# The order of two heads in the products of probabilities by values, in a two-block transformer forward pass

## Chip, cores and metric

The kernel runs on one core of one Trainium2 chip. The metric is the device time of one execution in microseconds (us). The engines are TensorE (PE, with its weight loads shown apart as PEld), VectorE (DVE), ScalarE (ACT), GpSimd (POOL) and SyncE (SP), which issues most of the transfers.

## The reference, cut to what matters

The model is a chain of four layers over 512 tokens of width 1024, all in float32. A gated delta rule with a mixture of experts comes first, then a sparse attention (here called the first attention block) with a mixture of experts, then two equal layers that each hold a latent attention, a spatial gating unit and a banded attention. All three attentions end in the same product, probabilities by values, for each head:

```
s = jnp.einsum('bqhd,bkhd->bhqk', qi, k).astype(jnp.float32) * scale
s = jnp.where(mask[None, None], s, NEG_INF_2)
p = jax.nn.softmax(s, axis=-1).astype(v.dtype)
return jnp.einsum('bhqk,bkhd->bqhd', p, v)
```

A head is 64 wide in the value, so two heads fill 128 partitions of an output. There are 16 heads in the first attention block (in 4 groups of 4, each with two branches that need softmax over tokens, br = 0 and 1), and 8 in each latent and each banded attention.

## The kernel before

Tokens are cut into NT = 4 tiles of 128. Weights come in pieces of 512 KB and are split on chip into a high and a low part (L107 on ACT, L108 on DVE), and a projection is three matmuls for each block of weights (L112, L113, L114 in `mm3`). The tile that such a projection accumulates in carries the name mm or br, after its group of PSUM banks: four banks are called mm, two are called br, two are called tp.

`softmax_t` works on one head. For each of the four query tiles t it makes the scores (in the first attention block L1293 and L1294), takes the row's maximum on DVE (L1108), the exponential on ACT (L1110), scales on DVE (L1113 or L1115), transposes t + 1 blocks on PE (L187, tile tp) and copies them on ACT into PT (L1117). PT holds all probabilities of that head, transposed, and is three deep. Four mm banks serve the scores and the output of the product.

The product works on a pair of heads, u = 0 and u = 1, that share one PSUM bank `o`: head 0 writes its partitions 0 to 63 and head 1 partitions 64 to 127. For each key tile jt the rows of queries from jt on are taken, so the matmuls have 512, 384, 256 and 128 columns for jt = 0 to 3. Each such float32 matmul is two instructions in the trace, so a pair of heads has 16 instructions: 4 key tiles by 2 heads by 2. In the first attention block they are on L1299 (8 pairs by 2 branches, 16 groups, x256 instructions), in the other two attentions on L1578 (2 layers by 2 attentions by 4 pairs, 16 groups, x256). The first matmul of each head, at jt = 0, reads columns of PT that the last query tile writes, so it needs that head's whole softmax.

```
for jt in range(NT):
    for u_ in range(2):
        h = 2 * p + u_
        PE.matmul(o[u_ * 64:u_ * 64 + 64, jt * 128:], lhsT=vt[:, jt, h * 64:h * 64 + 64],
                  rhs=pt_rhs(PTs[u_], jt), start=jt == 0, stop=jt == NT - 1)
```

The program is written straight on, but a planner in the tile framework orders the instructions of each engine before the program runs. It goes by its own costs, takes what is ready, and among ready instructions the one that stands first in the program. In the trace the instructions on PE are mixed accordingly: between the scores and the transposes of a head there are pieces of projections that stand later in the program. In the latent attention `branch(0, p, ...)`, a gated projection, follows the product of pair p. In the banded attention the operands of the next pair, `banded(p + 1)`, stand between the softmax of a pair and its product for p < 3. In the first attention block only `queries(g + 1)`, for g < 3, is there to be mixed in, and a group of heads begins with the scores of compressed blocks (L1259, L1260, tile sc), a softmax over them (DVE L1269 to L1276, ACT L1271, tile pc), transposes, and the product that opens the output bank (L1284).

Of the kernel before, what the change touches and what calls it, by code (L numbers as in the profile page):

```python
# [19 lines left out]
T = 512  # L20
# [45 lines left out]
class Net:  # L66
# [24 lines left out]
    def chunk(self, src, n=RING, eng=None):  # L91
        """a piece of a weight, on chip as two float32r parts that sum to it"""
        nc = self.nc
        j, self.turn = self.turn, (self.turn + 1) % (RAW + len(self.more))
        raw = self.more[j - RAW] if j >= RAW else self.ring.tile([128, RING], F32, name="raw", tag="raw", bufs=RAW)
        nc.sync.dma_start(raw[:, :n], src)
        j, self.turn2 = self.turn2, (self.turn2 + 1) % (HL + len(self.pairs))
        if j >= HL:
            hi, lo = self.pairs[j - HL]
        else:  # L100
            hi = self.ring.tile([128, RING], F32R, name="hi", tag="hi", bufs=HL)
            lo = self.ring.tile([128, RING], F32R, name="lo", tag="lo", bufs=HL)
        self.split(hi[:, :n], lo[:, :n], raw[:, :n], eng)
        return hi, lo
# [11 lines left out]
    def phase(self, **banks):  # L116
        """PSUM banks by tag for the stretch of the program that follows"""
        if banks != self.banks:
            self.pool.close()
            self.banks = banks  # L120
            if banks:
                self.ps = self.pool.enter_context(self.tc.tile_pool(name="ps", bufs=1, space=bass.MemoryType.PSUM))
# [11 lines left out]
    def proj_t(self, chunks, xh, xl, evac, kt=8, tag="mm"):  # L134
        """y^T tiles of 128 columns by 512 tokens; chunks hold 4 k by 256 columns."""
        m = 0
        nk = kt // 4
        for p in range(len(chunks) // nk):
            pst = [self.psum(tag), self.psum(tag)]
            for kk in range(nk):  # L140
                hi, lo = self.chunk(chunks[p * nk + kk])
                for j in range(2):
                    for k in range(4):
                        s = slice(k * 256 + j * 128, k * 256 + j * 128 + 128)
                        kx = kk * 4 + k
                        self.mm3(pst[j], hi[:, s], lo[:, s], xh[:, kx], xl[:, kx], kx == 0, kx == kt - 1)
            for j in range(2):
                evac(m, pst[j])
                m += 1

    def proj_n(self, chunks, xh, xl, evac, kt=8, n=512, inner=None, early=False):
        """y tiles of 128 tokens by n columns; chunks hold 2 k by n columns. inner: the last block's token tiles
        end one after the other, and evac follows as many tiles behind; early: they start one after the other,
        as far as the weights' places go."""
        nk = kt // 2
        for b in range(len(chunks) // nk):
            pst = [self.psum() for _ in range(NT)]
            def part(t, kk, ch):
                hi, lo = ch
                for k in range(2):  # L160
                    kx = kk * 2 + k
                    ts = slice(t * 128, t * 128 + 128)
                    cs = slice(k * n, k * n + n)
                    self.mm3(pst[t][:, :n], xh[:, kx, ts], xl[:, kx, ts], hi[:, cs], lo[:, cs], kx == 0, kx == kt - 1)
            last = b == len(chunks) // nk - 1
            lag = NT
            m = HL if early and not b else 1
            if inner is not None and last:
                m, lag = nk, inner
            for k0 in range(0, nk, m):  # L170
                ks = range(k0, min(nk, k0 + m))
                ch = [self.chunk(chunks[b * nk + kk], 2 * n) for kk in ks]
                for t in range(NT):
                    for kk in ks:
                        part(t, kk, ch[kk - k0])
                    if t >= lag:
                        evac(b, t - lag, pst[t - lag][:, :n])
            for t in range(max(0, NT - lag), NT):
                evac(b, t, pst[t][:, :n])

    def transpose_tile(self, src, n, evac, tag="tp"):
        """n 128-wide blocks of src (128 rows) transposed, four to a bank; evac(first, count, psum)."""
# [7 lines left out]
    def to_xt(self, src, t, xh, xl, n=8, tag="tp"):  # L190
        """token tile t [128, n*128] -> columns t of xh/xl [128, n, 512]."""
# [11 lines left out]
    def deeper(self, pool, n):  # L203
        """n more places for split weights, in pool"""
# [6 lines left out]
    def longer(self, *tiles):  # L211
        """tiles as further places for weights in flight"""
# [4 lines left out]
    def rpow(self, out, in_):  # L217
        """out = in_ ** -0.5 (small tiles)."""
# [3 lines left out]
    def rows(self, src, n, tag, eng=None):  # L222
        """DRAM row [1, n] on every partition."""
# [4 lines left out]
    def rows_pe(self, src, tag):  # L228
        """rows, by the tensor engine"""
# [9 lines left out]
def gdn(net, xt, aside):  # L239
    """gated delta rule: returns (yh, yl), the operand of the output projection; aside(room) is work for its idle queues."""  # L240
# [4 lines left out]
    with ExitStack() as cx:  # L245
# [17 lines left out]
        def gate(p, tag="mm", more=lambda: None):  # L263
            """2 silu(z) of two heads, transposed"""
# [9 lines left out]
        with ExitStack() as c1:  # L274
# [13 lines left out]
            # decay and step of each token and head  # L288
# [31 lines left out]
            def conv_silu(c, ps, dst, eng):  # L320
                """dst = 2 silu(causal conv of 4 taps)"""
# [15 lines left out]
            def inv_norm(i, h, key, out):  # L337
                """out[:, h::8] = 1 / norm of head h's rows"""
# [7 lines left out]
            def k_head(h):  # L346
                """the strictly lower part of (beta k k^T) * decay of a head's chunks"""
# [28 lines left out]
            def later(f, lag):  # L376
                """f, once lag others have come after it"""
# [30 lines left out]
            # inverses of the unit lower triangular blocks of 32, then 64, then 128  # L408
# [96 lines left out]
        with ExitStack() as c2:  # L505
            p3 = c2.enter_context(tc.tile_pool(name="gdn3", bufs=1))
            def prep(t):
                """decays, and the operands that carry them"""
# [83 lines left out]
            def scaled(t, so, ops):  # L592
                """rows of the heads over their norms"""
# [14 lines left out]
            def output(t, y, yh, yl):  # L608
                """transposed, and gated by z"""
# [70 lines left out]
def mix_out(net, l, chunks, yh, yl, resid, rp, done):  # L680
    """LayerNorm(alpha * resid + y @ w); done(t, tile) gets each token tile"""
# [24 lines left out]
class Moe:  # L706
# [22 lines left out]
    def route(self, t, h):  # L729
        """h: token tile t after the LayerNorm; picks its experts and sends its rows to them"""  # L730
# [26 lines left out]
    def dispatch(self):  # L757
        """top-2 experts of the top group of each token; slots of the experts' first 128 tokens"""
# [15 lines left out]
        def first_max(src, n, oh):  # L774
            """src (n by 4) - max of four, the maximum negated; the one-hot of its first place into oh"""
# [9 lines left out]
        # the best two of every group, and the best group  # L785
# [18 lines left out]
        # columns: token and destination row of a slot, in parts that bfloat16 holds  # L804
# [31 lines left out]
    def overflow(self):  # L836
        """the experts of tokens beyond the first 128 of an expert, in tiles of 128"""
# [82 lines left out]
    def places(self):  # L920
        """room that is idle between the projection before and the end of the experts, for their weights"""
# [8 lines left out]
    def experts(self):  # L930
# [6 lines left out]
        def operand(e, n, tag, src):  # L937
            """n transposed blocks of an expert's rows as an operand, and the steps that make it, four blocks each"""
# [10 lines left out]
        def up(e, xh, xl, steps):  # L949
            """gated hidden rows; steps run between the pieces of the weights"""  # L950
# [46 lines left out]
    def combine(self, done):  # L997
        """LayerNorm(alpha * h + the experts' weighted rows) by token tiles, all over alpha"""
# [68 lines left out]
def bias_setup(net, room):  # L1067
    """the biases by distance, in DRAM: n_fwd from -527, s_fwd from -127 on. Made in room [16, 1712]"""
# [18 lines left out]
def toeplitz(net, pool, src, h, bufs=2):  # L1087
    """tiles[u][p, x] = src[h + u, p + x]: the bias of query p of a tile and the key x before the tile's end"""
# [6 lines left out]
def softmax_t(net, pool, score, tb, gate=None, scale=1.0):  # L1095
    """P^T of a head: P = softmax(scale * (scores + bias)) (* gate), causal by tiles of 128: block
    t + 3 j of the tile is key tile j by query tile t"""
# [28 lines left out]
def nsa(net, xt):  # L1126
# [4 lines left out]
    with ExitStack() as cx:  # L1131
# [88 lines left out]
        with ExitStack() as c2:  # L1220
# [3 lines left out]
            def queries(g):  # L1224
                """scaled queries of a group's heads, high parts on partitions 0-63, low on 64-127"""
# [12 lines left out]
            for g in range(4):  # L1238
# [11 lines left out]
                # compressed blocks: scores of four heads, transposed  # L1250
# [29 lines left out]
                for pr in range(2):  # L1280
# [5 lines left out]
                    for br in range(2):  # L1286
# [10 lines left out]
                        for jt in range(NT):  # L1297
                            for u in range(2):
# [56 lines left out]
class Second:  # L1355
# [8 lines left out]
    def pre(self, t, h, pool):  # L1364
        """rmsnorm of token tile t, transposed into the projections' operand"""
# [9 lines left out]
    def silu2(self, pool, dst, ps):  # L1375
        """dst = 2 silu(ps)"""
# [5 lines left out]
    def run(self, done):  # L1382
# [6 lines left out]
        with ExitStack() as cx:  # L1389
# [13 lines left out]
            def branch(n, p, y, emit, tag="br"):  # L1403
                """a quarter of branch n: its gated products' columns 256 p to 256 p + 255, transposed"""
# [15 lines left out]
            with ExitStack() as c0:  # L1420
                ap = c0.enter_context(tc.tile_pool(name="mla", bufs=1))
                # latent attention's operands
# [35 lines left out]
                def fetch(j):  # L1458
                    """a piece of the up projections; it stays while other weights pass"""
# [5 lines left out]
                def query(h):  # L1465
                    """operand of a head's queries, kept in DRAM"""
# [15 lines left out]
                def z_store(i, chunks, more):  # L1482
                    """2 silu of a gate's columns, kept in DRAM"""
# [7 lines left out]
                def keys(m):  # L1491
                    """keys of two heads, and a tile of all heads' values"""
# [27 lines left out]
            # spatial gating  # L1520
            ya = y_pair()
            with ExitStack() as c0:
# [28 lines left out]
                def mix(m, ps):  # L1551
                    """a quarter of the branch: its values mixed along the sequence, times u and the gate"""
# [17 lines left out]
            with ExitStack() as c2:  # L1570
                ap = c2.enter_context(tc.tile_pool(name="att", bufs=1))

                def pv_pair(PTs, vt, p, i, yf):
                    o = net.psum()
                    for jt in range(NT):
                        for u_ in range(2):
# [11 lines left out]
                def banded(p):  # L1588
                    """operands of two heads of the banded attention"""
# [179 lines left out]
```

## Time and profile before

| | |
|---|---|
| time, median of 3 runs | 2262.78 us (2261.91 to 2266.01) |
| span of the profiled execution, first to last instruction | 2254.8 us |
| between span and median | 8.0 us |
| PE busy | 2108.0 us, 93% |
| PE weight loads busy | 1665.8 us, 74% |
| DVE busy | 1409.0 us, 62% |
| ACT busy | 1127.9 us, 50% |
| chain that ended last: share of PE | 62% |

The profile was taken of one execution. The time of that execution with what lies around its span isn't given apart; the span and the median differ by 8.0 us, and that difference is taken as what lies outside. A time in a row of the timeline is the start of an instruction, counted from the span's start, then its duration. Instructions of one line that follow each other are merged, with their count as x14. Matmuls overlap in a pipeline, so what an instruction takes from PE is read from its start to the start of the next, not from its duration.

### The profile page before, as it was taken

What the parts mean: (1) busy time and instruction counts of PE and PEld (TensorE: products, weight loads), DVE (VectorE), ACT (ScalarE), POOL (GpSimd) and SP (SyncE); (2) the same over time, 40 slices, a digit from 0 to 9 for tenths busy, and PEclk for the clock granted to TensorE, in tenths of its full rate; (3) what the DMA queues carried; (4) which work ended last, traced back from release to release, by engine and by line L of the source; (5) the groups of instructions that cost most, each with busy time, mean ns of one, the idle gap of its engine ahead of it and who ended that gap; (6) DMA issues with size and microseconds to landing.
All of it is one profiled execution on the core that took longest, in us unless ns stands there. A gap on an engine that the chain in (4) does not pass through costs nothing.

```text
span 2254.8 us, 30278 instructions
## 1 busy us (share of the span) xinstructions
PE 2108.0 (93%) x10641; PEld 1665.8 (74%) x10641; DVE 1409.0 (62%) x2872; ACT 1127.9 (50%) x2252; POOL 374.1 (17%) x367
## 2 busy tenths in 40 slices
PE   8898987996999989699959999999999999999998
PEld 7777876775777756577747877777887887777786
DVE  6787666886538876678865645455447555455544
ACT  4536534885427766288734335455344333455433
POOL 4411013553200001255430010000101001000000
PEclk9999998998999999899979999999999999999999
DMA  5344436995431112689546537322535645533442
GB/s 202 98 133 118 155 142 243 344 366 186 136 116 58 43 38 87 232 293 366 202 166 181 185 116 202 122 103 94 187 101 175 203 149 147 160 119 101 146 150 76
DMA packets 133530, 363.03 MB, mean 161 GB/s; under 512 B 28742, under 2 KB 41462, under 8 KB 131580
## 3 DMA queue, kind: packets, MB, share of 16 engines
q1 hardware_dynamic: 80748, 272.72, 35.7%
q0 software_dynamic: 19168, 51.71, 6.4%
q10 hardware_dynamic: 33456, 36.59, 5.4%
q8 instruction: 86, 1.41, 0.2%
q14 instruction: 72, 0.59, 0.1%
HBM read 315.22 MB, written 62.51 MB: 168 GB/s over the span
## 4 chain that ended last, share of the span: by engine, by line
PE 62%; DMA 6%; DVE 6%; issue 4%; ACT 3%; POOL 1%; POOLq 0%; another core or an unknown queue 0%; DVEq 0%; SPq 0%; ACTq 0%
PE mm L112 10%; PE mm L113 10%; PE mm L114 10%; PE br L113 5%; PE br L112 5%; PE br L114 5%; PE tp L187 5%; PE mm L955 3%; PE mm L1299 2%; PE mm L1578 2%; ACT hi L107 2%; DVE lo L108 1%; DMA xh<-in_m_w_dram 1%; PE mm L1293 1%; PE mm L1176 1%
## 5 line engine op out<-in xcount | busy, mean ns | idle before, releaser
L108 DVE TENSOR_TENSOR lo<-raw,hi 128x1024 fp32r<-128x1024 f32 (+1 forms) x262 | 325.1, 1245 | 313.2 <-ACT hi L107 307.1
L107 ACT CAST hi<-raw 128x1024 fp32r<-128x1024 f32 (+1 forms) x268 | 279.8, 1048 | 433.7 <-PE br L113 150.1
L112 PE MATMUL mm<-xh,hi 128*128 128x512 f32 x688 | 272.4, 396 | 1.1 <-DVE acc L326 0.9
L113 PE MATMUL mm<-xl,hi 128*128 128x512 f32 x688 | 270.5, 393 | 0.0
L114 PE MATMUL mm<-xh,lo 128*128 128x512 f32 x688 | 269.7, 393 | 0.2 <-DVE lo L108 0.2
L112 PE MATMUL mm<-hi,xh 128*128 128x512 f32 (+1 forms) x480 | 190.2, 396 | 3.8 <-ACT xh L107 3.0
L114 PE MATMUL mm<-hi,xl 128*128 128x512 f32 (+1 forms) x480 | 189.4, 395 | 1.7 <-DVE xl L108 1.5
L113 PE MATMUL mm<-lo,xh 128*128 128x512 f32 (+1 forms) x480 | 188.7, 393 | 0.0
L112 PE MATMUL br<-xh,hi 128*128 128x512 f32 x464 | 184.8, 398 | 2.2 <-DVE tm L1563 1.9
L113 PE MATMUL br<-xl,hi 128*128 128x512 f32 x464 | 186.7, 402 | 0.0
L114 PE MATMUL br<-xh,lo 128*128 128x512 f32 x464 | 182.7, 394 | 0.0
L1110 ACT ACTIVATE s<-s,mx 128x128 f32<-128x128 f32 (+3 forms) x256 | 143.1, 561 | 21.7 <-DVE mx L1108 21.1
L112 PEld LDWEIGHTS mm<-xh,hi 128*128 128x128 f32 x688 | 130.5, 190 | 29.2 <-issue 1.7
L114 PEld LDWEIGHTS mm<-xh,lo 128*128 128x128 f32 x688 | 129.8, 189 | 28.1 <-DVE lo L108 1.2
L113 PEld LDWEIGHTS mm<-xl,hi 128*128 128x128 f32 x688 | 130.4, 190 | 26.6
L1117 ACT COPY PT<-tp 128x128 f32<-128x128 f32 (+3 forms) x256 | 102.9, 425 | 31.0 <-PE tp L187 30.0
L112 PEld LDWEIGHTS mm<-hi,xh 128*128 128x128 f32 x480 | 91.8, 191 | 24.9 <-ACT xh L107 5.1
L955 PE MATMUL mm<-hi,xeh 128*128 128x512 f32 x256 | 109.1, 426 | 0.0
L187 PE MATMUL tp<-call,s 128*128 128x128 f32 x640 | 107.8, 278 | 0.8 <-ACT PT L1117 0.4
L114 PEld LDWEIGHTS mm<-hi,xl 128*128 128x128 f32 x480 | 91.7, 191 | 22.4 <-DVE xl L108 4.6
L187 PEld LDWEIGHTS tp<-call,s 128*128 128x128 f32 x640 | 75.0, 140 | 41.5 <-ACT PT L1117 16.8
L113 PEld LDWEIGHTS mm<-lo,xh 128*128 128x128 f32 x480 | 91.8, 191 | 17.9 <-issue 0.2
(518 smaller groups left out, 4523.5 us busy)
## 6 DMA issues: line engine op xcount, KB each, us to landing
raw<-in_s_w_dram SPq DMA_DIRECT2D x128, 512.0 KB
raw<-in_g_w_dram SPq DMA_DIRECT2D x40, 512.0 KB
raw<-in_m_w_dram SPq DMA_DIRECT2D x40, 512.0 KB
xh<-in_m_w_dram SPq DMA_DIRECT2D x40, 512.0 KB
xl<-in_m_w_dram SPq DMA_DIRECT2D x40, 512.0 KB
raw<-in_n_w_dram SPq DMA_DIRECT2D x32, 512.0 KB
raw<-in_s_br_dram SPq DMA_DIRECT2D x24, 512.0 KB
qk<-qkd SPq DMA_DIRECT2D x16, 768.0 KB
```

What stands on the lines that cost most here:

```text
L107: self.nc.scalar.copy(hi, src)
L108: (eng or self.nc.vector).tensor_tensor(lo, src, hi.bitcast(F32), op=OP.subtract)
L112: mm(ps, lhsT=ah, rhs=bh, start=start, stop=False)
L113: mm(ps, lhsT=ah, rhs=bl, start=False, stop=False)
L114: mm(ps, lhsT=al, rhs=bh, start=False, stop=stop)
L187: self.nc.tensor.transpose(tp[:, j], src(b + j), self.ident)
L955: PE.matmul(pg, lhsT=a[:, c * 2 + k], rhs=b[:, k * 512:k * 512 + 512], start=c + n == 0, stop=c == 3 and n == 5)
L1110: S.activation(p[:, :n], s[:, :n], AF.Exp, bias=mx, scale=-1.0, accum_out=sm)
L1117: S.copy(PT[:, t:4 * t + 1:3], tp)
L1176: PE.matmul(hv, lhsT=raw[:, k * 128:k * 128 + 128], rhs=Xs[i][:, :, l:l + 481:16], start=l == 0, stop=l == 30)
L1299: PE.matmul(o[u * 64:u * 64 + 64, jt * 128:], lhsT=vv[:, jt, br * 256 + g * 64:br * 256 + g * 64 + 64], rhs=pt_rhs(PTs[u], jt), start=Fals ...
L1578: PE.matmul(o[u_ * 64:u_ * 64 + 64, jt * 128:], lhsT=vt[:, jt, h * 64:h * 64 + 64], rhs=pt_rhs(PTs[u_], jt), start=jt == 0, stop=jt == NT - 1)
```

## The change

In both places where probabilities are multiplied by values, the inner loop runs over the heads in the order 1, 0 instead of 0, 1. Every matmul stays what it was, with the same operands, bank and flags; within each key tile the second head's now comes first. The change also empties comments and documentation strings, line for line.

```diff
@@ nsa
                         for jt in range(NT):
-                            for u in range(2):
+                            for u in (1, 0):
                                 PE.matmul(o[u * 64:u * 64 + 64, jt * 128:],
@@ Second.run, pv_pair
                     for jt in range(NT):
-                        for u_ in range(2):
+                        for u_ in (1, 0):
                             h = 2 * p + u_
```

## Rows read from the trace of the kernel before

**Rows 1.** The page, span and busy time of TensorE.

```profile
span 2254.8 us, 30278 instructions
PE 2108.0 (93%) x10641; PEld 1665.8 (74%) x10641; DVE 1409.0 (62%) x2872; ACT 1127.9 (50%) x2252; POOL 374.1 (17%) x367
```

**Rows 2.** Busy time by stretch: attentions of the last two layers, first attention block.

```profile
core 0: us, PE busy (x) PEld busy (x) DVE busy (x) ACT busy (x) POOL busy (x), PEclk, DMA share, GB/s
1338.00:1600.00 262.00, 260.08 (x1295) 202.77 (x1294) 138.16 (x357) 126.54 (x279) 7.81 (x17) 1.00 0.42 138
1882.00:2150.00 268.00, 266.06 (x1320) 207.66 (x1319) 139.15 (x358) 128.03 (x281) 7.81 (x17) 1.00 0.44 138
695.00:890.00 195.00, 186.33 (x1004) 127.47 (x1003) 152.07 (x577) 144.72 (x422) 1.61 (x3) 0.98 0.09 31
```

**Rows 3.** Who waited for whom in 1338 to 1600, TensorE alone.

```profile
PE br L112 <- DVE tm L1563: 1.0, 1, 1.0
PE mm L112 <- DMA qk<-qkd: 0.8, 1, 0.8
```

**Rows 4.** The timeline of TensorE around the latent attention's second pair.

```profile
1376.90 0.27 PE L187 MATMUL tp<-call,s 128*128 128x128 f32 x1
1376.93 0.48 PE L114 MATMUL br<-xh,lo 128*128 128x512 f32 x1
...
1377.93 0.38 PE L187 MATMUL tp<-call,s 128*128 128x128 f32 x2
1378.24 1.07 PE L1578 MATMUL mm<-PT,vt 128*64 128x512 f32 x2
1379.25 0.98 PE L187 MATMUL tp<-call,s 128*128 128x128 f32 x7
...
1381.09 2.37 PE L1578 MATMUL mm<-PT,vt 128*64 128x512 f32 x14
1383.38 0.50 PE L113 MATMUL br<-xl,hi 128*128 128x512 f32 x1
```

**Rows 5.** The timeline of TensorE at the banded attention's first pair.

```profile
1477.04 2.37 PE L1578 MATMUL mm<-PT,vt 128*64 128x512 f32 x16
1479.35 0.50 PE L112 MATMUL br<-xh,hi 128*128 128x512 f32 x1
```

**Rows 6.** Timeline: first and last opening pairs, first block, then the later layers.

```profile
699.69 1.07 PE L1299 MATMUL mm<-PT,vv 128*64 128x512 f32 x2
...
880.01 1.07 PE L1299 MATMUL mm<-PT,vv 128*64 128x512 f32 x2
...
1361.02 1.07 PE L1578 MATMUL mm<-PT,vt 128*64 128x512 f32 x2
...
2118.26 1.07 PE L1578 MATMUL mm<-PT,vt 128*64 128x512 f32 x2
```

**Rows 7.** The chain that ended last in 695 to 890, by line.

```profile
by line: PE mm L1299 26.5%; PE tp L187 20.2%; PE mm L1293 9.0%; PE mm L1294 8.1%; ACT s L1110 3.9%; PE mm L1284 3.6%; ACT PT L1117 3.2%; DVE s L1108 2.5%; PE br L113 1.9%; PE br L114 1.9%; PE br L112 1.8%; PE mm L1259 1.6%; issue 1.5%; PE m
```

**Rows 8.** Busy time by stretch, the first attention block's four groups (columns: rows 2).

```profile
695.00:738.00 43.00, 42.93 (x244) 30.13 (x243) 36.37 (x141) 33.66 (x101) 0.00 (x0) 1.00 0.09 33
738.00:789.00 51.00, 50.92 (x280) 35.93 (x279) 41.77 (x155) 38.65 (x110) 0.00 (x0) 1.00 0.13 42
789.00:840.00 51.00, 44.03 (x239) 28.79 (x237) 42.05 (x151) 37.85 (x110) 0.00 (x0) 1.00 0.12 42
840.00:890.00 50.00, 48.44 (x245) 32.62 (x246) 31.88 (x133) 34.55 (x102) 1.61 (x3) 0.93 0.02 6
```

**Rows 9.** Waits in 695 to 890: total us, times, longest.

```profile
DVE s L1108 <- PE mm L1294: 19.5, 21, 4.2
...
PE tp L187 <- DVE pc L1276: 5.1, 2, 4.9
```

**Rows 10.** Busy time by stretch at the start of the last group (columns: rows 2).

```profile
834.63:840.16 5.53, 0.66 (x6) 0.45 (x5) 4.39 (x8) 1.25 (x2) 0.00 (x0) 1.00 0.00 0
840.42:847.25 6.83, 6.16 (x19) 4.29 (x18) 2.48 (x13) 2.76 (x8) 0.00 (x0) 0.50 0.00 0
```

## Prediction

> **What bounds the kernel now.** I read the page first. TensorE is busy 93% of a span of 2254.8 us and no other engine is over 62% [rows 1], so I look at what the change does to TensorE's own time and ask in which stretch that time sets the end.
>
> The second view is the busy time by stretch [rows 2]. In the two stretches with the attentions of the last two layers, TensorE is busy 260.08 of 262 us and 266.06 of 268 us, and DVE and ACT about half. Over the first of these the list of waits has two entries for matmuls, 1.0 and 0.8 us [rows 3]: there TensorE simply works through its queue. The first attention block is different. TensorE is busy 186.33 of 195 us, but DVE is at 152.07 us (78%) and ACT at 144.72 us (74%) [rows 2]; engines there feed each other in a ring.
>
> The third view is the timeline around the product that is changed, and it holds the point of the case. In rows 4 the 16 instructions of a pair of heads do not stand together. Two of them, with 512 columns, start at 1378.24. They are head 0's first key tile. Then come transposes and a projection, and at 1381.09 the other 14. The reason is in the code: head 0's probabilities are complete long before head 1's, and its first matmul stands first in the loop, so the planner sends it ahead into a place where head 1's softmax isn't ready. The second matmul of the loop is head 1's, needs head 1's whole softmax, and all others wait behind it.
>
> Now the price of that. The opening pair runs alone and takes 1.01 us, from 1378.24 to the next start at 1379.25. The other 14 take 2.29 us (1381.09 to 1383.38) [rows 4]. At the first banded pair the 16 stand together, and all of them take 2.31 us (1477.04 to 1479.35) [rows 5]. Two more instructions of 512 columns thus cost 0.02 us there. Head 0 and head 1 write different halves of the output's partitions, and the trace shows that matmuls of the two halves run side by side; the opening pair is dear only because it has no partner.
>
> The split is in 26 of the 32 groups: in all 16 of the first attention block, the first at 699.69 and the last at 880.01, and in 10 of 16 later on, from 1361.02 to 2118.26, namely all four latent pairs and the last banded pair of each layer [rows 6]. In the other six, the next pair's projection stands ahead of the product in the program and takes the free place.
>
> **The change, part by part.** No instruction is added or removed, and no transfer moves, so SP's and POOL's queues keep what they have. What changes is which matmul stands first. It is now head 1's, which needs the softmax that comes last. Head 0's first matmul cannot go ahead of it, if the planner keeps the order of the matmuls into one bank. It does so now: head 0's second key tile is as ready as its first, and in none of the 26 groups has it gone ahead of head 1's first. So I expect 32 groups of 16, at about 2.31 us.
>
> *One split undone.* The last transpose before the opening pair starts at 1378.04 (1377.93 and one step of 0.11), and the pair 0.20 us later; after a transpose at 1376.90 a projection's matmul starts 0.03 us later [rows 4]. So the split costs 0.20 + 1.01 - 0.03 = 1.18 us of TensorE. The group of 16 gives back 0.02. That is 1.16 us for each, and with the pair's own 1.01 alone 0.99.
>
> *The ten later groups.* TensorE waits for nothing in these stretches, and the projections that stand behind can take the place. What hides nothing now can hide nothing later: 10 x 1.16 = 11.6 us, and 9.9 at the lower price. The product ends no later against the other work of TensorE, and DVE, at 138.16 of 262 us [rows 2], has room.
>
> *The sixteen groups of the first block.* All of it is at most 16 x 1.16 = 18.6 us, and at least nothing, if TensorE only waits in place of the opening pair. For much speaks the chain that ended last: L1299 has 26.5% of it in this stretch, 51.7 us [rows 7], nearly all of the 16 x (1.01 + 2.29) = 52.8 us that the products take. So the opening pair delays what comes after it. Also, DVE's maximum waits 19.5 us in sum for the scores [rows 9], and scores that come earlier are what it wants. Against all of it speaks DVE. Each quarter of the stretch holds four groups, so 4.6 us could go, and DVE is busy 36.37 of 43, 41.77 of 51, 42.05 of 51 and 31.88 of 50 us [rows 8]. If DVE can be busy no more than the 84.6% of the first quarter, the quarters get down to 43, 49.4, 49.7 and, untouched by that bound, 45.4: a gain of 0 + 1.6 + 1.3 + 4.6 = 7.5 us. At 90% it is 2.6 + 4.6 + 4.3 + 4.6 = 16.1. I take 87%, since part of DVE's waits end with the split: quarters of 41.8, 48.0, 48.3 and 45.4, a gain of 1.2 + 3.0 + 2.7 + 4.6 = 11.5 us.
>
> The sum is 11.6 + 11.5 = 23.1 us off. The profiled execution's 2254.8 us of span become 2231.7. The median of the runs shown lies 8.0 us above that span; I leave this difference as it is, and 2262.8 becomes 2239.7 us.
>
> A rule speaks against the second term. The Trainium skill, in Perfetto Trace Analysis, section Identifying the Most-Contended Engine, says that the busy share of matmuls is no good measure of how near TensorE is to its limit, since pipelined matmuls hide small gaps, and that the share of weight loading is a better one. By that measure the first block is at 127.47 of 195 us, 65%, and the later stretches at 77% [rows 2]. Read so, TensorE has slack in the first block, and the sum would be the first term alone, 11.6 us. The trace speaks partly against it, since the opening pairs stand on the chain [rows 7].
>
> **The rivals.** The first is that the first block gives nothing. TensorE would stand idle where the opening pair stood, because the next transposes wait for DVE's scaling and the next scores for a free bank. Then only the ten later groups count, and the time is 2251 to 2253 us. The unequal load of TensorE and DVE speaks for it: DVE is busy 36.37 of 43 us in the first quarter [rows 8]. The chain speaks against.
>
> The second rival gives the gain back at one place. When a group of heads begins, its small softmax over compressed blocks leaves TensorE without work of the block itself. At the last such place, after 834.63, TensorE is busy 0.66 of 5.53 us, and then the granted clock is 0.50 for 6.83 us, which is 1.2 GHz [rows 10]. That is 4.9 us idle, 3.4 us lost at half the clock and 0.7 us more of idle time within it, 9 us. At the two places before it, around 738 and 788, nothing of the kind shows (busy 50.92 of 51 us between them [rows 8]), because projections of queries fill them. These are limited in number. If the planner, with the opening pairs gone, uses them up earlier, one such place left empty costs 9 us and two cost 18. With one, the sum is 23.1 - 9 = 14.1 and the time 2248.7, still faster. With both, and the block's own gain kept, it is 2257.7. It ends slower if both are empty and the sixteen groups give back less than 18 - 11.6 = 6.4 of their 18.6 us; with nothing given back the time is 2269 us. For it speaks that the planner goes by its own costs and will redraw the whole block. Against it, that opening pairs stand mostly where no projection was ready.
>
> The third is that the change doesn't do what it says: the planner sees two halves of a bank as independent, and head 0's four matmuls go ahead. The time would be the same or worse. That none does so now leaves little to it.
>
> **How the numbers follow.** The main case gets 0.68. Its own range runs from 9.9 + 7.5 = 17.4 us off to 30.2 off, if all 26 splits pay in full: 2232.6 to 2245.4 us. The first rival gets 0.16, the second 0.12 (0.05 of it slower by more than the bound, 0.04 within it, 0.03 faster), the third 0.03, half of it within the bound, half slower. The last 0.01 is a gain beyond the full price. The bound within which I call it the same is 0.2%, 4.5 us, about what a measurement of this kernel can tell from no change. Faster is 0.68 + 0.16 + 0.03 + 0.01 = 0.88, the same 0.055 and slower 0.065, which I round to 0.06 each. The range reaches from the full gain with a little to spare, 2231, to beyond the first rival, 2254; the cases inside hold about 0.85.
>
> **What would show it.** If I am right, the profile after has 32 groups of 16 on L1299 and L1578, none of 2 and 14, each about 2.31 us from its start to the next line's. The stretch from the start of a later layer's attentions to their end is shorter by about 5 x 1.16 = 5.8 us, and the first block by about 11. TensorE's busy time falls by less than 27 us and the span by about 23. I am wrong on the first term if the later layers' stretches lose less than 4 us each; on the second, if new waits of transposes for DVE or of L1299 for the copies into PT show in the first block, or if idle time and a granted clock of 0.50 stand at the start of its second or third group of heads.

## The result, and the profile after

The changed kernel takes 2234.6 us (median, 2228.09 to 2240.57) against 2262.35 us for the kernel before: a ratio of 0.9878 with a 95% interval of 0.9859 to 0.9896, so 23.5 to 31.9 us less. The forecast was 2239.7 us, within 2231 to 2254.

The page of the changed kernel begins so (compare [rows 1]):

```profile
span 2226.3 us, 30272 instructions
PE 2077.6 (93%) x10641; PEld 1649.4 (74%) x10641; DVE 1407.0 (63%) x2872; ACT 1127.0 (51%) x2252; POOL 374.1 (17%) x367
```

The same number of matmuls ran, x10641, and the span is 28.5 us shorter. The time of this profiled execution is 2228.09 us, 1.8 us over its span; the 8.0 us that the forecast left between span and median [rows 1] was thus mostly the difference between one execution and the median.

TensorE's timeline at the product that ends the first group of heads and around the latent attention's second pair, which answers to [rows 4]:

```profile
729.99 0.60 PE L187 MATMUL tp<-call,sc 128*128 128x128 f32 x4
730.35 0.48 PE L114 MATMUL br<-xh,lo 128*128 128x512 f32 x1
730.83 2.38 PE L1299 MATMUL mm<-PT,vv 128*64 128x512 f32 x16
...
1361.91 2.38 PE L1578 MATMUL mm<-PT,vt 128*64 128x512 f32 x16
1364.21 0.50 PE L114 MATMUL br<-xh,lo 128*128 128x512 f32 x1
```

All 32 groups are of 16 now, and the opening pair is gone everywhere. A group takes 2.30 us from its start to the next line's (1361.91 to 1364.21); behind the one that ends the third group of heads TensorE stands idle.

Where did 28.5 us go? Busy time by stretch, first block from its first L1284 to the end of its last product, changed kernel, with the columns of [rows 2]; the second line is the same stretch of the kernel before:

```profile
691.28:867.91 176.63, 168.14 (x1002) 116.83 (x1002) 149.60 (x582) 141.82 (x423) 0.00 (x0) 1.00 0.11 35
```

```profile
691.81:885.63 193.82, 185.14 (x1000) 126.37 (x1000) 152.03 (x582) 143.56 (x423) 0.00 (x0) 0.98 0.10 32
```

The first block lost 17.2 us. For the later layers I take the time from the first product of the gating unit to the first operand after all three branches. Timeline, kernel before and then changed:

```profile
1326.34 0.44 PE L1560 MATMUL br<-wsT,vl 128*64 128x128 f32 x4
...
1653.18 0.62 ACT L1664 ACTIVATE xh<-mg 128x512 fp32r<-128x512 f32 x1
```

```profile
1308.48 0.44 PE L1560 MATMUL br<-wsT,vl 128*64 128x128 f32 x4
...
1629.80 0.62 ACT L1664 ACTIVATE xh<-mg 128x512 fp32r<-128x512 f32 x1
```

That is 326.84 us before and 321.32 after, 5.5 less; the second of the two layers, measured between the same instructions, lost 5.4. With 0.5 us ahead of the first block these make 28.6. That the two profiles start their first block at nearly the same time, 691.81 and 691.28, is luck: in the 14 profiles of this case it starts between 690.25 and 698.72, after a stretch that no kernel here changes. So the later layers gave 10.9 us where the sum had 11.6, and the first block 17.2 where it had 11.5.

The granted clock is part of that. In the kernel before it was 0.50 for 6.83 us when the last group of heads began, after 4.9 us of idle time [rows 10]. In the changed kernel the idle time there is about half as long, and the clock stays at 1.00 through the rest of the block:

```profile
824.92:827.22 2.30, 0.07 (x3) 0.03 (x1) 2.23 (x6) 0.62 (x1) 0.00 (x0) 1.00 0.01 4
828.52:867.91 39.39, 37.75 (x225) 25.35 (x225) 29.24 (x129) 30.58 (x98) 0.00 (x0) 1.00 0.00 1
```

Half of 6.83 us is 3.4 us. It leaves 13.8 us for the sixteen splits of the first block. Half is an estimate, which takes all of that time for TensorE's. The profiles of kernels without splits suggest less: against the changed kernel's 176.63 us, the block takes 1.4 us more in `first_block_only` and 1.2 more in `changed_again`, each with 3.4 us at 0.50, and 2.3 more in `softmax_swapped_old_order` with 6.8 us. At 2.3 us for the clock the splits have 14.9.

### The profile page after: what moved, and what is told of

The parts are those of the page before. It is cut to its first block, busy times and chain, and to the rows that moved or that the text cites. A ratio compares the mean times of both kernels' runs of the same rounds, so it can differ in the third digit from the quotient of the medians.

```text
span 2226.3 us, 30272 instructions
## 1 busy us (share of the span) xinstructions
PE 2077.6 (93%) x10641; PEld 1649.4 (74%) x10641; DVE 1407.0 (63%) x2872; ACT 1127.0 (51%) x2252; POOL 374.1 (17%) x367
## 4 chain that ended last, share of the span: by engine, by line
PE 47%; DMA 3%; DVE 3%; issue 2%; ACT 2%; POOL 1%; SPq 0%; DVEq 0%; POOLq 0%; ACTq 0%
PE mm L112 8%; PE mm L113 8%; PE mm L114 8%; PE br L112 5%; PE br L114 5%; PE br L113 5%; PE tp L187 3%; PE mm L955 2%; PE mm L1578 2%; ACT hi L107 1%; DMA raw<-in_m_w_dram 1%; DMA qk<-qkd 1%; DVE lo L108 0%; PE mm L1642 0%; PE mm L1641 0%
## 5 line engine op out<-in xcount | busy, mean ns | idle before, releaser
L1117 ACT COPY PT<-tp 128x128 f32<-128x128 f32 (+3 forms) x256 | 103.1, 425 | 23.8 <-PE tp L187 23.3
L187 PE MATMUL tp<-call,s 128*128 128x128 f32 x640 | 107.4, 277 | 2.0 <-ACT PT L1117 0.9
L112 PEld LDWEIGHTS br<-xh,hi 128*128 128x128 f32 x464 | 87.2, 188 | 21.0 <-issue 3.2
```

Source lines behind the costliest of these rows:

```text
L112: mm(ps, lhsT=ah, rhs=bh, start=start, stop=False)
L187: self.nc.tensor.transpose(tp[:, j], src(b + j), self.ident)
L1117: S.copy(PT[:, t:4 * t + 1:3], tp)
```

## Experiments

**One place at a time.** The changed kernel, with the old order put back in one of the two places.

```diff
 first_block_only, pv_pair
-                        for u_ in (1, 0):
+                        for u_ in range(2):
 later_layers_only, nsa
-                            for u in (1, 0):
+                            for u in range(2):
```

> The new order in the first attention block alone (L1298), the old one in the latent and banded attentions. If the places add up as the trace of the changed kernel has them, the sixteen groups of the first block stand together and give about 17 us against the kernel before, and the ten later splits of 2 and 14 are back: near 2245. If the first block's gain was luck of the whole plan, or came from the clock in one run, it gives 11 us or less: 2251 or more.

> The new order in the latent and banded attentions alone (L1576), the old one in the first block. Ten splits undone at 1.16 us: 11.6 us less than before, near 2251, and the stretch of each later layer about 5 us shorter. If TensorE's freed time were lost in new waits there, under 4 us, near 2260. The sum of this and the run with the first block alone should be the whole change's 27 us; if it is far from it, the two places act on each other.

The first block alone takes 2246.15 us against 2261.85, a ratio of 0.9928 (0.9914 to 0.9941): 16 us less. The later layers alone take 2250.52 us, 0.9951 (0.9938 to 0.9965): 11 us less. The two add up to the whole change's 27.

**Readiness or halves.** Both orders of the products, with the softmaxes of a pair made in the other order.

```diff
-                        PTs = []
-                        for u in range(2):
+                        PTs = {}
+                        for u in (1, 0):
...
-                            PTs.append(softmax_t(...))
+                            PTs[u] = softmax_t(...)
 (the same in the latent and the banded attention)
```

> The products keep the old order, head 0 first, but in all three attentions the softmax of head 1 is made before that of head 0. If what counts is that the first matmul of the loop needs the softmax that comes last, the 16 instructions stand together in 32 groups and the time is that of the changed kernel, 2235. If it is the half of the bank that is written first, it is as slow as before, 2262, with 26 splits.

> The changed order of the products, head 1 first, and head 1's softmax made before head 0's. If readiness counts, the first matmul of the loop is ready early again, 26 groups are split into 2 and 14, and the time is that of before, 2262. If the order of the halves counts, it stays at 2235.

With the old order of the products it takes 2236.98 us (0.9885, 0.9866 to 0.9903), as fast as the changed kernel. With the changed order it takes 2264.18 us (1.0016, 1.0004 to 1.0027), as slow as the kernel before. Its trace has 28 splits, 16 in the first block and 12 later, two more than expected. Its first group, on TensorE's timeline, is split again, though head 1's half is written first:

```profile
700.87 1.07 PE L1299 MATMUL mm<-PT,vv 128*64 128x512 f32 x2
701.87 0.44 PE L1294 MATMUL mm<-kl,qst 128*128 128x384 f32 x1
```

So what counts is whether the first matmul of the loop needs the softmax that comes first or last.

**Where the first block's gain sits.** Much of it shows where a group of heads begins. From the last product of a group to the next L1284 the kernel before takes 9.82, 10.42 and 9.35 us, the changed one 6.85, 6.90 and 5.90: 9.9 us in three places, where the whole block lost 17.2. The changed timeline above shows why one might stop here: the transposes of the compressed scores (tile sc, 729.99) now stand ahead of the product, and the chain of the small softmax runs beside it. I formed a second theory from that, that the four groups that end a group of heads pay most, and a rival to the even price of each split.

```diff
 ends_only, nsa (later layers as before)
-                            for u in (1, 0):
+                            for u in ((1, 0) if pr == 1 and br == 1 else (0, 1)):
 not_ends, nsa (later layers as before)
-                            for u in (1, 0):
+                            for u in ((0, 1) if pr == 1 and br == 1 else (1, 0)):
```

> The new order only in the four groups of the first attention block that end a group of four heads (pr = 1 and br = 1); the old order in the other twelve and in the later layers. If each undone split pays the same, 4 x 1.16 = 4.6 us less than before, near 2257. If the first block's gain sits mostly where a group of heads begins, because the transposes of the compressed scores now come before the last product and not behind it, these four pay about 10 us, near 2252, and the time from the start of that product to the start of the next group's L1284 falls from about 10 us to about 7.

> The complement within the first block: the new order in the twelve groups that do not end a group of heads, the old one in the four that do and in the later layers. If each pays the same, 12 x 1.16 = 13.9 us less than before, near 2248. If the gain sits at the starts of the groups of heads, about 6 us, near 2256, with 9 to 10 us from the last product to the next L1284 as before.

The second theory fell. The four groups alone give 2258.87 us, 0.9982 (0.9972 to 0.9992), 4 us; the other twelve give 2251.14 us, 0.9953 (0.9940 to 0.9966), 11 us. The three places take 7.79, 6.53 and 9.61 us with the four ends undone, 5.7 us less in sum than before, and 7.75, 7.74 and 9.59 with the other twelve undone, 4.5 us less, though no split at the end of a group is undone there. The table has the first block, from its first L1284 to the end of its last product, in the profiles of the kernels; the last column takes off half of the time that the granted clock stood at 0.50 within it.

| kernel | splits in the first block | block, us | at 0.50, us | block less half of that, us |
|---|---|---|---|---|
| before | 16 | 193.8 | 6.8 | 190.4 |
| later_layers_only | 16 | 193.6 | 6.8 | 190.2 |
| ends_only | 12 | 190.5 | 6.8 | 187.1 |
| not_ends | 4 | 184.0 | 6.8 | 180.6 |
| first_block_only | 0 | 178.1 | 3.4 | 176.4 |
| changed | 0 | 176.6 | 0 | 176.6 |

Undoing the four ends is worth 3.2 us and undoing the other twelve 9.7, 0.81 us each both times, among four kernels with the same 6.8 us at 0.50. All 16 are worth 13.8 us, 0.86 each, or 14.9 and 0.93 if the clock's part is 2.3 us. So the block's length goes by the number of splits. The other profiles with the compressed blocks in their place and the halves side by side, read like the last column, give 176.6, 176.1 and 175.5 us without splits and 191.6 with 16 (`softmax_swapped_new_order`, 10.2 us at 0.50): one profile tells the block to about 1 us. The time that shows at the starts of the groups of heads is thus not what the splits there cost: with the four ends undone 5.7 us show there and the block is 3.2 shorter, and with the other twelve undone 4.5 us show there all the same.

**The same question from the other side.** The compressed blocks of the next group of heads are made right after its queries.

```diff
-            nq = queries(0)
+            def compressed(g, qs):
+                ...  # the lines from bt to pcT, moved
+                return pcT
+            nq = queries(0)
+            npc = compressed(0, nq)
...
                         nq = queries(g + 1)
+                        npc = compressed(g + 1, nq)
```

> The changed kernel with the scores, softmax and transposes of the compressed blocks of the next group of heads written right after its queries, ahead of the last two softmaxes and products of the group before. TensorE should no longer idle at the start of a group: the 6 to 7 us from the last product to L1284 shrink to about 3, and with three such places it is 9 to 12 us faster than the changed kernel, near 2225. If that chain only takes DVE's time from the other softmaxes, it is no faster, 2235 or more.

> The same move of the compressed blocks in the kernel before. If the order of the heads gains 10 us in the first block only by letting that chain start earlier, the move takes this part away: against the same move with the new order it is slower by the later layers' 11 us and some 6 more, about 17, near 2242. If the order gains the same everywhere, the two are 27 us apart, near 2252.

They take 2227.09 us (0.9852, 0.9838 to 0.9867) and 2255.66 us (0.9968, 0.9957 to 0.9980). The ratios are 0.0116 apart, 26 us, near the 27 of an even price and far from 17. Their profiles are 29.7 us apart in span: 12.6 us in the block (172.38 against 184.98), 13.5 in the two later layers, 2 of which go with a fall of the clock that only the slower profile has there, and 4.8 ahead of the block, where the two kernels are the same, less 1.2 elsewhere. From the last product of a group to the next L1284 the new order takes 3.15, 4.28 and 13.25 us, so only the first two places shrank as expected. Whether the move makes the changed kernel faster was tried once more, side by side.

> The changed kernel once more, to stand beside the next one on the same chip: 2235, within 2230 to 2241. If runs in which the granted clock falls once more or once less in the first block make the spread, the span and the mean granted clock of the single runs go together, 3.4 us for each fall of 6.8 us at half.

> The changed kernel with the early compressed blocks once more, beside it. If the 7 us between the two medians are the idle time at the starts of the groups of heads, it is faster by 4 to 9 us here too, near 2228; if they were the difference between two chips, the two agree within 3 us.

They took 2231.19 us (0.9881, 0.9860 to 0.9903) and 2229.26 us (0.9861, 0.9842 to 0.9880). The block is 177.81 and 172.47 us in their profiles, but the medians are 1.9 us apart and the intervals overlap. That the move beats the changed kernel is not shown. In these profiles its block is 5.3 us shorter, but the stretch ahead of the block is 4.7 us longer (the block starts at 690.55 and 695.26) though the kernels are the same there. On single runs the expectation held in part: over the eight runs of the changed kernel the mean granted clock falls from 0.974 to 0.968 as the span grows from 2226.3 to 2238.8 us, and four falls of 6.8 us at 3.4 us each, an estimate, would be 13.6 of these 12.5 us. That the falls lie in the first block is not shown, since only a profile tells their place; and among the runs of other kernels the order does not always hold (`later_layers_only`: 2247.8 us at 0.970, 2251.1 us at 0.971).

**Side by side.** Two kernels change only the order inside a group.

```diff
 first_tile_swapped, both places
-    for u in (1, 0):
+    for u in ((1, 0) if jt == 0 else (0, 1)):
 halves_one_after_other, both places
-    for jt in range(NT):
-        for u in (1, 0):
+    for u in (1, 0):
+        for jt in range(NT):
```

> Head 1 first in the first key tile alone, head 0 first in the other three, in all attentions. Only the first matmul of a group can be sent ahead, so this should hold all 32 groups together and give the changed kernel's time, 2235. If the order inside the later key tiles matters for how well the two halves run side by side, a group of 16 takes longer than 2.31 us, and each 0.1 us more is 3 us of time.

> All four key tiles of head 1, then all four of head 0, in all attentions: the 16 instructions stay together but no matmul has a partner in the other half of the output next to it. If running side by side is what makes the group cheap, it takes about twice 2.2 us in place of 2.31, some 2.1 us more for each of 32 groups, and 2235 becomes about 2300. If the opening pair was dear only for the change of the array's shape and back, a group stays near 2.3 us and the time near 2235.

The first takes 2234.14 us (0.9892, 0.9875 to 0.9908): its trace has 32 groups of 16, and the order in the first key tile is all of the change. The second takes 2279.68 us (1.0085, 1.0068 to 1.0102), 45.5 us more than the first on the same chip. Its 16 instructions stand together, but in TensorE's timeline a group takes 3.86 us (1375.45 to 1379.31), not 2.30:

```profile
1375.45 3.93 PE L1578 MATMUL mm<-PT,vt 128*64 128x512 f32 x16
1379.31 0.51 PE L113 MATMUL br<-yl,hi 128*128 128x512 f32 x1
```

I had put 2.1 us more on each group and it is 1.56, so the expected 2300 us was too high; of 32 x 1.56 = 49.9 us, 45.5 came out. The halves are not quite one after the other either. Between 1377.18 and 1377.20 two matmuls of this group run, one of 256 columns and one of 512:

```profile
L1578 PE MATMUL mm<-PT,vt x2: 379/512/644, 1377.0 to 1377.0; 128*64 128x256 f32 x1, 128*64 128x512 f32 x1
```

The one of 512 is the first of head 0, which starts at 1377.01, 1.56 us after the group, beside head 1's third key tile. From there to the end, 1379.31, head 0's eight instructions take 2.30 us, as long as all 16 in pairs. So a half alone takes as long as both together. That is also why the 14 that stayed behind an opening pair saved nothing: they hold one head's eight instructions whole. This kernel also gives a second measure of how TensorE's time turns into the block's. Its first block takes 201.05 us, with 3.4 at 0.50; less half of that 199.4, which is 22.9 us more than the 176.5 of the last two rows of the table. TensorE's own extra there is 16 x 1.56 = 25.0 us. In busy time, with the columns of [rows 2]:

```profile
692.97:894.02 201.05, 193.01 (x996) 129.50 (x997) 150.52 (x582) 142.61 (x423) 0.00 (x0) 0.99 0.10 31
```

DVE's 150.52 us are what they always are (149.60 in the changed kernel); only TensorE's work and the length moved.

## Why the prediction was right

**What bounds.** That the later layers are paced by TensorE alone held: of 11.6 us for ten splits, 10.9 came out in the profile and 11 in the run with the later layers alone.

**One split undone.** The mechanism held in each part. The planner keeps the order of the matmuls into a bank, so nothing goes ahead any more; groups of 16 take 2.30 us; the swapped softmaxes show that readiness makes the split; and the halves one after the other show that the opening pair was dear because it had no partner. The price of 1.16 us was a little high. It took 0.03 us as the step that stays without the pair, from a transpose to a projection, but behind this pair stand transposes [rows 4], and two transposes are 0.11 us apart (1377.93, two in 0.38 us of 0.27 each). That makes 1.08 us. Transposes follow seven of the ten later pairs, so the ten come to some 11 us, which is what came out.

**The first block.** The direction held, the size and its parts were off: the term of 11.5 us measured 13.8 from the splits, or 14.9, and 17.2 in the profile with the clock's part. The step that was mis-sized is the bound by DVE, by which it may be busy 87% at most. By groups of heads, from one L1284 to the next and the last to the end of the last product, the kernel before and then the changed one have

```profile
691.81:741.35 49.54, 49.40 (x273) 34.81 (x273) 41.31 (x154) 36.93 (x109) 0.00 (x0) 1.00 0.14 49
741.35:792.81 51.46, 50.58 (x277) 35.69 (x277) 42.48 (x156) 39.32 (x111) 0.00 (x0) 1.00 0.13 42
792.81:841.68 48.87, 41.95 (x228) 27.31 (x228) 38.79 (x145) 35.96 (x107) 0.00 (x0) 0.99 0.10 33
841.68:885.63 43.95, 43.22 (x223) 28.55 (x223) 29.44 (x129) 31.35 (x98) 0.00 (x0) 0.94 0.00 1
```

```profile
691.28:737.67 46.39, 46.36 (x278) 33.80 (x278) 40.94 (x155) 37.48 (x109) 0.00 (x0) 1.00 0.17 52
737.67:784.80 47.13, 45.39 (x272) 32.51 (x271) 41.82 (x156) 38.42 (x111) 0.00 (x0) 1.00 0.14 46
784.80:828.52 43.72, 38.64 (x228) 25.17 (x229) 37.60 (x145) 35.34 (x106) 0.00 (x0) 1.00 0.11 37
```

and 39.39 us in the last (828.52, above). DVE is at 88%, 89% and 86% in the changed kernel, over what I allowed in the first two. The gains are 3.2, 4.3, 5.2 and 4.6 us; less half of the time at 0.50 in the kernel before, 0.6 us in the third group and 2.8 in the last, they are 3.2, 4.3, 4.5 and 1.8. The forecast had 1.2, 3.0, 2.7 and 4.6. So the three groups that DVE was to limit gave more, and the last, which it was not to limit, gave less. That the sum came within a few us is in part luck, because the two errors offset each other.

The runs show little of a limit by DVE. TensorE's idle time in the block, its length less the busy time, was 8.7 us before (193.82 less 185.14) and is 8.5 now (176.63 less 168.14), though in the last group it rose from 0.7 to 1.6. The new waits that would have been a sign against the second term are small: transposes wait 0.6 us for DVE's scaling (L187 for L1115), and the weight loads of L1299 wait 4.0 us for the copies into PT (L1117), 5.0 before. Of the waits for DVE, that of the scores' weight loads for the maximum (L1293 for L1108) grew most, from 4.5 to 6.4 us. Nor does a split pay less the more of them are undone, as a limit would have it. Why a split is worth 0.81 to 0.93 us in this block and 1.09 in the later layers stays open.

One sign did not come out as forecast: TensorE's busy time fell by 30.4 us, more than 27. The first block has 17.0 of it, and there 6.16 us of the time before had passed at half the clock [rows 10]; the two later layers have some 11.

**The rivals.** The first block gave 16 us by itself, so the rival in which it gives nothing fell. The Trainium skill's rule, in Perfetto Trace Analysis, section Identifying the Most-Contended Engine, that weight loading shows TensorE's nearness to its limit better than matmuls do, would have left the first block out; weight loads are at 66% of the block in the changed kernel (116.83 of 176.63 us), and yet 22.9 of 25.0 us of added matmul time came out in the block's length. As a sign of what paces this block, the measurement decides against the rule. The reason on that page is that pipelined instructions look smaller in the trace; the small gaps that the prediction names are not in its words. The second rival, idle time at the starts of groups of heads, went the other way: those places got shorter, and at the last of them, after 2.2 us of idle time each, the clock fell for 0, 0, 3.4, 3.4 and 6.8 us in the five profiles that have no splits in the first block, groups of 2.30 us and the compressed blocks where they were, against 6.8 us after 4.9 in the four kernels of the table that have splits in the block. The third rival, that head 0 goes ahead anyway, did not occur.

**What the 5 us of distance are.** The first block's splits gave 2.3 us more than their term, or 3.4. Against that block alone, 16 us in the medians, the splits' 13.8 or 14.9 us leave 1 to 2 us for the clock, which I had counted only as a risk. The later layers gave 0.7 us less. Together 23.1 becomes some 27 us; the rest is within the spread of the medians.

## What to carry to other kernels

Where two matmul streams run side by side in the two halves of one output, let the loop begin with the stream whose operand is ready last, or a planner that takes what is ready will send the first matmul ahead alone. What stays behind then takes no less time, because the other half alone takes as long as both. Before calling such early work free, look for what runs right behind it: in a stretch where TensorE never waits, a gap that is filled is not a gap. And where a stretch gets shorter, the place at which the time shows is not its cause; making the change at that place alone, and then everywhere else alone, tells it.

## What the runs showed of the hardware that was not expected

Float32 matmuls of 64 output columns in the two halves of an output run side by side at no price that shows: 16 instructions in pairs take 2.30 us, and one half's eight alone take 2.30 us as well (1377.01 to 1379.31). The clock came in as a second effect of the first: at the last group of heads, 4.9 us of idle time ended in 6.83 us at 0.50 [rows 10], and the shorter idle time at the same place, 2.2 us in each of five profiles without splits, in none, 3.4 or 6.8 us.
